# A two-layer backbone kernel on one core: work of the rounds moved from VectorE to GpSimd, convolution steps dealt out anew, two sets of weights placed elsewhere

## The chip, the core and the metric

The kernel runs on one core of one Trainium2 chip. Its five engines run side by side, each through its own list of instructions: TensorE (PE in the profile; its weight loads are PEld), VectorE (DVE), ScalarE (ACT), GpSimd (POOL) and SyncE (SP), which here issues nearly all DMA transfers. An instruction that needs another engine's result waits for a semaphore, and everything behind it on its engine waits with it.

The metric is the device time of one execution in microseconds. The kernel before takes 1331.81 us (median of three: 1330.71, 1331.81, 1332.05).

## The reference, cut to what matters

One sample: x is 1024 tokens by 1024 features, ctx 256 tokens by 1024. All inputs are 32-bit floats. Layer 0 works on x and on ctx, layer 1 on x alone.

```python
def even_mixer(h, h0, p):                        # layer 0
    z = h @ p["w_in"]                            # 1024 -> 5 x 1024
    va, vg, ga, xb, gb = jnp.split(z, 5, axis=-1)
    y_a = conformer_conv(va, vg, p) * silu(ga)
    y_b, hT = rglru_branch(xb, p, h0, True)
    y_b = y_b * silu(gb)
    return concatenate([y_a, y_b], -1) @ p["w_out"], hT

def conformer_conv(va, vg, p):
    u = va * sigmoid(vg)
    u = depthwise_conv(u, conv_w, conv_b)        # 31 taps along the tokens
    return silu(layernorm(u, ln_g, ln_b))        # over the features

def rglru_branch(xb, p, h0, with_outputs):
    u = depthwise_conv(xb, sconv_w, sconv_b)     # 4 taps
    # both directions: r, i = sigmoid(block-diagonal products of u)
    # a = exp(-8 r softplus(-lam)); b = sqrt(1 - a^2) * i * u
    # h[t] = a[t] h[t-1] + b[t]; y = forward h + backward h

# layer 0: x = x + gate * even_mixer(modulate(rmsnorm(x)), states of ctx)
# layer 1: a pooling mixer with gates; then a last rmsnorm
```

## The kernel before, in words

**Layout.** Features lie on the 128 partitions, tokens along the free axis, so 1024 features are eight tiles j = 0 to 7 of 128 x 1024. Halves of 512 tokens (h = 0, 1) are the unit of one PSUM bank. ctx adds 256 columns to the tiles of the recurrent branch, hence the shapes 128x1280.

**Products.** Each float32 factor is split into a high part (a cast on ACT; names with h, as `wh_vg`, `ybh`, `uh`) and a low part (value minus high part, a subtraction; names with l, as `wl_vg`, `ybl`, `ul`). A product is three matmul series, high by high, low by high and high by low. PE needs each low part one matmul after the high part, so a late low part stops it.

**What sets the order.** From the start of layer 0 to the end of its convolution branch every engine's order is written by hand: the helper `on` (L471 to L476) chains each instruction behind the one before it on its engine, and all of them carry the line L475 in the profile. Behind that (from L1147 on) a scheduler sets the order from its own estimate. The profile's lines tell the two apart.

**The rounds (L703 to L799).** Round j, for j = 0 to 7, takes 42.5 us. On PE: vg(j), va(j), the next tile's xb, the block-diagonal gate products `g`, all from the normalised input. On ACT the sigmoids, exponentials, square roots and the high parts of the weights. On GpSimd the low parts of the weights (`wl_vg`, `wl_va`, `wl_xb`, `wl_gw`) and the element products of the recurrence (`l<-l,uc`, `l<-l,l`). On DVE the four-tap convolution of xb (`uc<-xb,sm,uc`), u = va * sigmoid(vg), the scans of the tile before (`rec_scan`: an element-wise step and two scans for each direction, all `l<-l,l`), the sum of both directions (`rec_sum`, 128x1024), and the long convolution.

**The long convolution** of tile j (`conv(j)`) is a generator of some 50 steps, most of them one SCALAR_TENSOR_TENSOR over half the tokens ("a tap"). Its two accumulators `conv` lie in PSUM banks; the rows with `wsum` use sums of neighbouring tokens (`cL`, made by `spread_sum`, or in place for j of 5 and more). The eight tiles have 395 steps. They have no place of their own: `fill(n)` puts the next n steps at the point of the DVE order where it is called. When a tile is done, `ln_sums` adds it to `lnsum`, two 128x512 additions, for the mean of the layernorm. Before the change a full round calls for 30 steps, the gap behind the last round for 26, the gated tiles for 46, and what is then left runs in the stretch of the wob products.

**Last scans (L836 to L851).** Products gb1 to gb3 run on PE while the last tile is scanned; the low part of the weights gb4 is made on DVE between the two scans.

**Gated tiles (L982 to L1008).** For each tile n and half h: `yr` (the recurrence's output, from DRAM) times the silu of gb (`sb`) on DVE, the high part `ybh` on ACT, the low part `ybl` on GpSimd, then some taps on DVE. `gb_weights(j + 2)` puts a weight's load, cast and low part between tiles: gb5 to gb7, then the first two of w_out's lower half (`wob` 0 and 1).

**wob products (L1061 to L1091).** For m = 0 to 7, two halves each: 48 matmuls over the eight gated tiles. m = 0 takes tiles 0 to 6 of both halves first, then tile 7. Behind each half DVE has `fill(7)`. After m = 5 PE takes the layernorm's mean, a product of `lnsum` with ones (`mu`, `ln_mean`), for which all eight convolutions must be done; at m = 6 and 7 DVE centres the tiles, adds up squares, and PE makes `ms_ln`.

**ya and woa (L1147 on).** Scheduled: the gate products ga, the multiplication with u, four combinations of quarters (`ya_t1`, `ya_t2`, `ya_b11`, `ya_b21` and three more), and then w_out's upper half by a scheme of seven products of quarters in place of eight (`quad`, L937ff: in order b11, t1, t2, b21, t3, b22, t4, with psum names qa, qc, qb). Its weights are combined likewise in `wquad` (loads `wr_woa`, sums `ws_woa` and L912, L913, L919, splits `wq_woa`).

## Time and profile before

| | |
|---|---|
| median of three runs | 1331.81 us |
| the profiled execution's own time | 1331.6 us |
| its span (first to last instruction) | 1329.8 us |
| mean granted clock of TensorE | 0.986 |
| TensorE busy | 1282.6 us, 96% of the span, 5600 matmuls |
| VectorE busy | 1139.7 us, 86%, 1771 instructions |
| ScalarE busy | 631.0 us, 47% |
| GpSimd busy | 320.6 us, 24%, 172 instructions |

How to read it. A row of the timeline gives the start in us from the span's start, the duration, the engine, the line, the operation and its tiles (out<-in), the shape, "xN" where N like rows follow each other and are shown as one, and in brackets how long the engine had been idle before it and what ended that. Matmuls are pipelined: each is shown with 0.39 us, but at full clock they start 0.227 us apart, so it is the distance of the starts that counts on PE. The same goes for DVE and GpSimd, where a row's end overlaps the next row's start by about 0.08 us. In the table of windows each stretch of time has the busy time of PE, PEld, DVE, ACT and POOL with the number of instructions, the granted TensorE clock, the share of the DMA engines and GB/s.

### The profile page before, as it was taken

Reading aid. Unit: us, or ns where it says so; the run is one execution under the profiler, and the core shown is the slowest. Engines: PE = TensorE matmul, PEld = TensorE weight load, DVE = VectorE, ACT = ScalarE, POOL = GpSimd, SP = SyncE. Lnnn points to the kernel's source line nnn. Section 1 sums busy time; section 2 is a strip of 40 time slices with the busy share of each in tenths; the row PEclk is TensorE's granted clock in tenths of the full one; section 3 lists DMA queues with packets and bytes.
Section 4 is the critical chain, followed back from the end, with each engine's and each line's share of the span. In section 5 each row is a group of like instructions: output and inputs, shape, how many; then the busy total and the mean of one; then the engine's idle time right before and its main releaser. Section 6 shows DMA issues by size and latency. Waiting matters only on the chain. (4 is left out here: it accounts for less than half of the span.)

```text
span 1329.8 us, 15728 instructions
## 1 busy us (share of the span) xinstructions
PE 1282.6 (96%) x5600; PEld 1026.3 (77%) x5600; DVE 1139.7 (86%) x1771; ACT 631.0 (47%) x919; POOL 320.6 (24%) x172
## 2 busy tenths in 40 slices
...
GB/s 360 345 117 145 56 55 49 56 56 72 40 64 51 100 107 125 172 96 80 167 190 182 120 192 188 88 127 151 118 112 111 117 113 166 261 222 256 214 100 127
DMA packets 82867, 181.80 MB, mean 137 GB/s; under 512 B 7778, under 2 KB 27618, under 8 KB 82788
## 3 DMA queue, kind: packets, MB, share of 16 engines
...
HBM read 136.72 MB, written 44.04 MB: 136 GB/s over the span
## 5 line engine op out<-in xcount | busy, mean ns | idle before, releaser
L475 DVE SCALAR_TENSOR_TENSOR conv<-u,sm,conv 128x505 f32<-128x505 f32 (+6 forms) x224 | 153.1, 746 | 0.8
L1582 POOL TENSOR_TENSOR o<-x,rr 128x256 f32<-128x256 f32 (+1 forms) x9 | 8.0, 927 | 460.6 <-ACT rr L1570 460.6
L475 ACT ACTIVATE l<-g,sm 128x512 f32<-128x512 f32 (+1 forms) x96 | 58.7, 619 | 57.8 <-PE g L475 56.0
L281 PE MATMUL fold<-graw,wu 128*128 128x512 f32 x128 | 57.4, 609 | 1.6 <-DMA wu<-wu 1.6
L475 POOL TENSOR_TENSOR l<-l,l 128x1280 f32<-128x1280 f32 x16 | 47.1, 2961 | 26.1 <-DVE conv L475 21.1
L475 PE MATMUL wob<-ybl,wh_wob 128*128 128x512 f32 x128 | 50.6, 395 | 2.4 <-POOL ybl L475 2.4
L475 PE MATMUL wob<-ybh,wh_wob 128*128 128x512 f32 x128 | 51.6, 403 | 0.0
L281 PEld LDWEIGHTS fold<-graw,wu 128*128 128x128 f32 x128 | 24.8, 195 | 33.5 <-issue 29.6
L475 PE MATMUL wob<-ybh,wl_wob 128*128 128x512 f32 x128 | 50.4, 394 | 0.0
L475 PE MATMUL gb<-h0l,wh_gb 128*128 128x512 f32 x128 | 49.8, 389 | 0.0
L475 PE MATMUL gb<-h0h,wh_gb 128*128 128x512 f32 x128 | 49.8, 389 | 0.0
L475 PE MATMUL vg<-h0h,wh_vg 128*128 128x512 f32 x128 | 49.8, 389 | 0.0
L475 PE MATMUL vg<-h0h,wl_vg 128*128 128x512 f32 x128 | 49.8, 389 | 0.0
L475 PE MATMUL vg<-h0l,wh_vg 128*128 128x512 f32 x128 | 49.8, 389 | 0.0
L475 PE MATMUL va<-h0h,wh_va 128*128 128x512 f32 x128 | 49.8, 389 | 0.0
L475 PE MATMUL va<-h0l,wh_va 128*128 128x512 f32 x128 | 49.8, 389 | 0.0
L475 PE MATMUL va<-h0h,wl_va 128*128 128x512 f32 x128 | 49.8, 389 | 0.0
L475 PE MATMUL gb<-h0h,wl_gb 128*128 128x512 f32 x128 | 49.8, 389 | 0.0
L102 ACT CAST wq_g<-wr_g 128x512 fp32r<-128x512 f32 x48 | 28.2, 620 | 45.1 <-DVE wr_g L912 18.3
L475 DVE TENSOR_TENSOR_SCAN l<-l,l 128x256 f32<-128x256 f32 (+1 forms) x32 | 48.7, 1521 | 1.1
L102 ACT CAST wq_wo<-wr_wo 128x512 fp32r<-128x512 f32 x48 | 28.9, 620 | 40.5 <-DMA wr_wo<-wo 13.8
L475 DVE SCALAR_TENSOR_TENSOR conv<-cL,wsum,conv 128x506 f32<-128x506 f32 (+3 forms) x70 | 47.6, 746 | 0.2
...
## 6 DMA issues: line engine op xcount, KB each, us to landing
...
```

The lines of the kernel that those rows point to most:

```text
L102: return (nc.scalar.copy(hi, src), eng.tensor_tensor(out=lo, in0=src, in1=hi.bitcast(F32), op=sub))
L281: nc.tensor.matmul(ps, w[:, kc], gs[i], start=(i == 0), stop=(i == 3))
L475: last[eng] = f(*args, **kw)
L1582: nc.gpsimd.tensor_tensor(out=o[:, k - k0], in0=v, in1=rr, op=mult)
```

## The change

Five edits. **(1)** In the rounds three groups of SBUF-only work go from DVE to GpSimd: `ul`, the low part of the convolved tile, in all eight rounds; `rec_sum` in seven rounds (the last stays on DVE); and the `ln_sums` of tiles that end within the rounds, which are now called ahead of `rec_exp`. `at_rest` (the `cL` sums) is called before the scans and no longer calls `ln_sums`. **(2)** The calls of `fill` in a round go from 2, 2 and 4 to 3, 4 and 8 (5 in the last round); 10, 6 and 3 stay. **(3)** At the last scans `fill(24)` becomes `fill(15)`, and `ln_sums` follows `rec_sum`. **(4)** The low parts `ybl` go from GpSimd to DVE, with one tap between the cast's input and the subtraction; the taps behind each half go from 2, 2, 4, 4, 4, 4, 3, 0 to 1, 1, 2, 2, 2, 2, 1, 0, so that with the new tap the gated tiles have 38 instead of 46; and the weights wob 1 come behind tile 6 instead of ahead of it. **(5)** `wquad_begin` starts the weights of the first woa block ahead of the last ga product: both loads, the sums and two splits there, the other splits at the old place.

```diff
@@ -581,11 +581,14 @@
     ended, summed, spread_ = [0], [1], [0]
     NSPREAD = 5
 
-    def ln_sums():
+    def vadd(**kw):
+        return vec(nc.vector.tensor_tensor, **kw)
+
+    def ln_sums(by=vadd):
         for j in range(summed[0], ended[0]):
             for h in range(2):
                 first = us[0][:, HALF[h]] if j == 1 else lnacc[h][:, :H]
-                vec(nc.vector.tensor_tensor, out=lnacc[h][:, :H], in0=first, in1=us[j][:, HALF[h]], op=add)
+                by(out=lnacc[h][:, :H], in0=first, in1=us[j][:, HALF[h]], op=add)
         summed[0] = max(summed[0], ended[0])
 
     def edge_sum(j):
@@ -604,7 +607,6 @@
         return cL[:, HALF[j % 2]]
 
     def at_rest():
-        ln_sums()
         while spread_[0] < min(whole_[0], ended[0] + 2, NSPREAD):
             spread_sum()
 
@@ -679,9 +681,9 @@
             vec(nc.vector.tensor_tensor_scan, out=iu[:, lat], data0=at[:, lat], data1=iu[:, lat],
                 initial=first, op0=mult, op1=add)
 
-        def rec_sum(st):
+        def rec_sum(st, by):
             hs, hb = st[2][1], st[2][3]
-            vec(nc.vector.tensor_tensor, out=hs[:, C:], in0=hs[:, C:], in1=hb[:, C:], op=add)
+            by(out=hs[:, C:], in0=hs[:, C:], in1=hb[:, C:], op=add)
             nc.sync.dma_start(yb_raw[st[0]], hs[:, C:])
 
 
@@ -718,7 +720,7 @@
             all_of(mm3_fixed(vg[0], w, (hh, hl), HALF[0]))
             if state is not None:
                 rec_input(state, 1)
-            fill(2)
+            fill(3)
             first_tap(j, xb, uc[:, C:])
             other_taps(j, xb, uc[:, C:], 1)
             if state is not None:
@@ -730,8 +732,8 @@
             uh, ul = utile(f"uh{j}", F32R), utile(f"ul{j}", F32R)
             cast(uh, uc)
             act(sg[1], vg[1], AF.Sigmoid)
-            fill(2)
-            vec(nc.vector.tensor_tensor, out=ul, in0=uc, in1=uh.bitcast(F32), op=sub)
+            fill(4)
+            gp(out=ul, in0=uc, in1=uh.bitcast(F32), op=sub)
             name = "gb0" if final else f"xb{j + 1}"
             wnext = raw_split(raw_load(win[4 * KT] if final else win[3 * KT + j + 1], name), name)
             gwh, gwl = [tpool.tile([P, H], F32R, tag="t", name=f"w{n}_gw{j}") for n in "hl"]
@@ -748,6 +750,7 @@
                 vec(nc.vector.tensor_tensor, out=m0[:, 0, 2 * KT :], in0=m0[:, 0, 2 * KT :],
                     in1=col(O_MB + 2 * KT, KT), op=add)
             if state is not None:
+                ln_sums(gp)
                 rec_exp(state)
                 rec_root(state)
                 for d in range(2):
@@ -773,11 +776,11 @@
             fill(3)
             if not final:
                 other_taps(j + 1, xc, ucn[:, :C])
+            at_rest()
             if state is not None:
                 for d in range(2):
                     rec_scan(state, d)
-                rec_sum(state)
-            at_rest()
+                rec_sum(state, gp)
             xb = wide(name if final else f"xb{j + 1}")
             steps = (x for h in range(2) for x in mm3_fixed(xb[:, HALF[h]], wnext, (hh, hl), HALF[h]))
             if state is None:
@@ -795,7 +798,7 @@
                     w = raw_split(raw, name)
                     rec_input(now, 0)
             all_of(steps)
-            fill(19 if state is None else 4)
+            fill(19 if state is None else 5 if final else 8)
             state, uc = now, ucn
 
 
@@ -838,7 +841,7 @@
         gb_silu(0)
         gb_silu(1)
         gb_product(3, gws[3])
-        fill(24)
+        fill(15)
         rec_scan(state, 0)
         raw = raw_load(win[4 * KT + 4], "gb4")
         hi = wpool.tile([P, D], F32R, tag="wh", name="wh_gb4")
@@ -847,7 +850,8 @@
         vec(nc.vector.tensor_tensor, out=lo, in0=raw, in1=hi.bitcast(F32), op=sub)
         gws[4] = hi, lo
         rec_scan(state, 1)
-        rec_sum(state)
+        rec_sum(state, vadd)
+        ln_sums()
         at_rest()
 
     cpool.release()
@@ -889,6 +893,34 @@
     loaded = [None]
 
 
+
+    def wquad_begin(src, name, ring):
+        raw = []
+        for i in range(2):
+            r = wpool.tile([P, D], F32, tag="wr", name=f"wr_{name}_{i}")
+            loaded[0] = nc.sync.dma_start(r, src[i])
+            raw.append(r)
+        a11, a12 = [raw[0][:, h] for h in HALF]
+        a21, a22 = [raw[1][:, h] for h in HALF]
+
+        def op(v, i):
+            t = ring(f"wq_{name}_{i}")
+            split(v, t[:, HALF[0]], t[:, HALF[1]], nc.vector)
+            return t
+
+        s3 = ttile(f"ws_{name}")
+        nc.vector.tensor_tensor(out=s3, in0=a11, in1=a21, op=sub)
+        nc.vector.tensor_tensor(out=a21, in0=a21, in1=a22, op=add)
+        p1, p5 = op(a11, 1), op(a21, 5)
+        nc.vector.tensor_tensor(out=a11, in0=a21, in1=a11, op=sub)
+
+        def rest():
+            p6, p2, p7 = op(a11, 6), op(a12, 2), op(s3, 7)
+            nc.vector.tensor_tensor(out=a12, in0=a12, in1=a11, op=sub)
+            p3 = op(a12, 3)
+            return p1, p2, p3, op(a22, 4), p5, p6, p7
+
+        return rest
 
     def wquad(src, name, ring, late=False):
         raw = []
@@ -986,25 +1018,28 @@
             nc.sync.dma_start(y, yb_raw[n][:, HALF[h]])
             vec(nc.vector.tensor_tensor, out=y, in0=y, in1=sbs[n][h], op=mult)
             cast(th[:, HALF[h]], y)
-            gp(out=tl[:, HALF[h]], in0=y, in1=th[:, HALF[h]].bitcast(F32), op=sub)
+            fill(1)
+            vec(nc.vector.tensor_tensor, out=tl[:, HALF[h]], in0=y, in1=th[:, HALF[h]].bitcast(F32), op=sub)
             fill(between)
         bh.append(th)
         bl.append(tl)
 
     gb_product(4, gws[4])
-    gated(0, 2)
+    gated(0, 1)
     gb_silu(2)
     gb_weights(5)
     gb_product(5, gws[5])
-    gated(1, 2)
+    gated(1, 1)
     for j in range(3, KT + 1):
         if j < KT:
             gb_silu(j)
-        if 3 < j < KT:
+        if 3 < j < KT - 1:
             gb_weights(j + 2)
         if 3 < j < KT - 2:
             gb_product(j + 2, gws[j + 2])
-        gated(j - 1, (0, 0, 4, 4, 4, 4, 3, 0)[j - 1])
+        gated(j - 1, (0, 0, 2, 2, 2, 2, 1, 0)[j - 1])
+        if j == KT - 1:
+            gb_weights(j + 2)
         ln_sums()
 
 
@@ -1140,6 +1175,14 @@
 
     mods = mod_halves()
 
+    ring_n = 0
+
+    def ring_w(name):
+        nonlocal ring_n
+        tag = ("wh", "wl", "d", "d")[ring_n % 4]
+        ring_n += 1
+        return dtile(name, F32R) if tag == "d" else wpool.tile([P, D], F32R, tag=tag, name=name)
+
     ya = {}
     for name in BOPS[:4]:
         operand(ya, name, d2tile, "ya")
@@ -1147,6 +1190,8 @@
     for i in range(KH):
         for j in (i, KH + i) if i else ():
             w = wload(win[2 * KT + j], f"ga{j}", nc.gpsimd)
+            if j == KT - 1:
+                w0 = wquad_begin([wout[q, 0] for q in range(2)], "woa0", ring_w)
             for h in range(2):
                 ps = psum(f"ga{j}_{h}")
                 mm3(ps, w, (hh, hl), HALF[h])
@@ -1169,18 +1214,10 @@
         for _ in range((6, 6, 4, 0)[i]):
             next(mods)
 
...
-    w0 = wo_weights(0)
+    w0 = w0()
     for name in BOPS[4:]:
         operand(ya, name, dtile, "ya")
         for i in range(KH):
```

Three places where instructions move. First, GpSimd in round 4, from `wl_va` to the next tile's `wl_vg`; `l<-l,l` with 128x1280 are the recurrence's products, and numbers behind names are the program's own. Before:

```order
L475 TENSOR_TENSOR wl_va_2109<-wr_va_2106,wh_va_2108 128x1024
L475 TENSOR_TENSOR wl_xb_2149<-wr_xb_2146,wh_xb_2148 128x1024
L475 TENSOR_TENSOR wl_gw_2153<-wr_gw_2154,wh_gw_2152 128x512
L475 TENSOR_TENSOR l_658<-l_658,l_653 128x1280
L475 TENSOR_TENSOR l_657<-l_657,l_654 128x1280
L475 TENSOR_TENSOR wl_vg_2369<-wr_vg_2235,wh_vg_2368 128x1024
```

With the change:

```order
L475 TENSOR_TENSOR wl_va_2133<-wr_va_2130,wh_va_2132 128x1024
L475 TENSOR_TENSOR ul_2164<-uc_1949,uh_2163 128x1280
L475 TENSOR_TENSOR wl_xb_2175<-wr_xb_2172,wh_xb_2174 128x1024
L475 TENSOR_TENSOR wl_gw_2179<-wr_gw_2180,wh_gw_2178 128x512
L475 TENSOR_TENSOR l_658<-l_658,l_653 128x1280
L475 TENSOR_TENSOR l_657<-l_657,l_654 128x1280
L475 TENSOR_TENSOR l_658<-l_658,l_657 128x1024
L475 TENSOR_TENSOR wl_vg_2398<-wr_vg_2262,wh_vg_2397 128x1024
```

`ul` now stands ahead of `wl_xb`, and the 128x1024 sum of both directions between the recurrence's products and `wl_vg`.

Second, the last gated tiles: GpSimd before, from tile 5's second low part to tile 7's (`wl_wob` are the low parts of the weights wob 0 and wob 1):

```order
L475 TENSOR_TENSOR ybl_3937<-yr_1_3948,ybh_3936 128x512
L475 TENSOR_TENSOR wl_wob_3968<-wr_wob_3965,wh_wob_3967 128x1024
L475 TENSOR_TENSOR ybl_3972<-yr_0_3973,ybh_3971 128x512
L475 TENSOR_TENSOR ybl_3972<-yr_1_3981,ybh_3971 128x512
L475 TENSOR_TENSOR ybl_3990<-yr_0_3991,ybh_3989 128x512
L475 TENSOR_TENSOR ybl_3990<-yr_1_3996,ybh_3989 128x512
```

DVE with the change, tile 6 (`yr_0_3998`) and the first half of tile 7:

```order
L475 TENSOR_TENSOR yr_0_3998<-yr_0_3998,sb_0_3962 128x512
L475 SCALAR_TENSOR_TENSOR conv_0_3694<-u_2870,wsum 128x512
L475 TENSOR_TENSOR ybl_3997<-yr_0_3998,ybh_3996 128x512
L475 SCALAR_TENSOR_TENSOR u_2870<-u_2870,sm,conv_1_3695 128x512
L475 TENSOR_TENSOR yr_1_4005<-yr_1_4005,sb_1_3963 128x512
L475 SCALAR_TENSOR_TENSOR conv_1_3695<-u_2870,wsum,conv_1_3695 128x511
L475 COPY conv_1_3695<-edges 128x1
L475 TENSOR_TENSOR ybl_3997<-yr_1_4005,ybh_3996 128x512
L475 SCALAR_TENSOR_TENSOR conv_0_3694<-u_2870,wsum,conv_0_3694 128x505
L475 TENSOR_TENSOR yr_0_4021<-yr_0_4021,sb_0_3992 128x512
L475 SCALAR_TENSOR_TENSOR conv_1_3695<-u_2870,wsum,conv_1_3695 128x506
L475 TENSOR_TENSOR ybl_4020<-yr_0_4021,ybh_4019 128x512
```

The low parts of tile 6 stood on GpSimd behind those of wob 1; they now stand on DVE, one tap behind the product that they come from.

Third, DVE ahead of the first woa block, from the sum behind t1 on. `u*ga` is L1155 before and L1200 now, the sums of the weights L911 to L919 before and L912 to L919 now. Before:

```order
L103 TENSOR_TENSOR ya_t1l_4873<-u_1831,ya_t1h_4871 128x512
L1155 TENSOR_TENSOR u_3158<-u_3158,ga_0_5351 128x512
L103 TENSOR_TENSOR ya_b21l_4881<-u_3158,ya_b21h_4879 128x512
L1155 TENSOR_TENSOR u_3158<-u_3158,ga_1_5378 128x512
L1162 TENSOR_TENSOR u_1831<-u_3158,u_1831 128x512
L1163 TENSOR_TENSOR yat_3_5409<-u_3158,u_1831 128x512
L911 TENSOR_TENSOR ws_woa_5425<-wr_woa_0_5418,wr_woa_1_5420 128x512
L1164 TENSOR_TENSOR u_3158<-u_3158,yat_3_5409 128x512
L912 TENSOR_TENSOR wr_woa_1_5420<-wr_woa_1_5420 128x512
L103 TENSOR_TENSOR ya_t2l_4877<-yat_3_5409,ya_t2h_4875 128x512
L103 TENSOR_TENSOR wq_woa_7_5438<-ws_woa_5425,wq_woa_7_5438 128x512
L913 TENSOR_TENSOR wr_woa_0_5418<-wr_woa_1_5420,wr_woa_0_5418 128x512
```

With the change:

```order
L103 TENSOR_TENSOR wq_woa_5_5361<-wr_woa_1_5353,wq_woa_5_5361 128x512
L1200 TENSOR_TENSOR u_3210<-u_3210,ga_0_5365 128x512
L103 TENSOR_TENSOR ya_t1l_4873<-u_1853,ya_t1h_4871 128x512
L103 TENSOR_TENSOR wq_woa_6_5432<-wr_woa_0_5351,wq_woa_6_5432 128x512
L103 TENSOR_TENSOR wq_woa_2_5435<-wr_woa_0_5351,wq_woa_2_5435 128x512
L103 TENSOR_TENSOR wq_woa_4_5445<-wr_woa_1_5353,wq_woa_4_5445 128x512
L103 TENSOR_TENSOR ya_t3l_5450<-u_847,ya_t3h_5448 128x512
L103 TENSOR_TENSOR ya_t3l_5450<-u_1172,ya_t3h_5448 128x512
L919 TENSOR_TENSOR wr_woa_0_5351<-wr_woa_0_5351 128x512
L103 TENSOR_TENSOR ya_b21l_4881<-u_3210,ya_b21h_4879 128x512
```

The two sums that open the weights (`ws_woa`, L913) and the third (L915) stand ahead of the first of these rows now, wq_woa_5 ahead of the last tile's products, and the weights 6, 2 and 4 with two low parts of t3 ahead of `ya_b21l`; the products that end in `ya_t2l` come later. On PE the first block's steps of b11 and t1 keep their places; then came two steps of t2, two of b21 and ten of t2, and now come nine of t2, twelve of b21, two of the next block's b11, one of t2 and twelve of b22.

6 lines of the change are left out of this document (removed).

## The prediction

> **What bounds the kernel now.** PE is busy 96% of the span, so I read the table of PE's waits first, then the windows, which tell in which stages PE works without a gap, then the timelines around the longest waits.
>
> ```profile
> PE mu L475 <- DVE lnsum L475: 10.1, 1, 10.1
> ...
> PE qc_woa L931 <- ACT wq_woa L102: 2.5, 1, 2.5
> PE wob L475 <- POOL ybl L475: 2.4, 1, 2.4
> ```
>
> ```profile
> core 0: us, PE busy (x) PEld busy (x) DVE busy (x) ACT busy (x) POOL busy (x), PEclk, DMA share, GB/s
> ...
> 245.00:290.00 45.00, 45.00 (x223) 38.20 (x223) 41.81 (x57) 26.46 (x30) 22.68 (x10) 1.00 0.15 53
> ...
> 706.00:760.00 54.00, 51.00 (x212) 41.15 (x211) 44.04 (x71) 25.70 (x47) 0.00 (x0) 0.94 0.52 176
> ```
>
> Each of the three waits occurs once and lies where the change works. In the window of a round PE has no gap at all: nothing is to be won there, only lost. DVE is idle for 45.00 - 41.81 = 3.2 us of it, GpSimd for 22.3 us. So the rounds can carry more of DVE's work, if it stays inside those idle times.
>
> What each wait costs is read from the starts of matmuls, since the clock falls behind a stop. First wait, the gated tiles' low part:
>
> ```profile
> 513.73 0.39 PE L475 MATMUL wob<-ybh,wh_wob 128*128 128x512 f32 x1
> 516.49 0.50 PE L475 MATMUL wob<-ybl,wh_wob 128*128 128x512 f32 x1 [2.37 <-POOL ybl L475]
> ...
> 517.77 0.63 PE L475 MATMUL wob<-ybh,wh_wob 128*128 128x512 f32 x1
> ...
> 521.16 0.40 PE L475 MATMUL wob<-ybh,wl_wob 128*128 128x512 f32 x1
> ```
>
> There are 14 steps from 513.73 to 521.16, 7.43 us. At 0.227 us a step (further down, 609.08 to 609.31) they take 3.18. Loss: **4.25 us**, of which 2.5 is the stop and the rest the slow steps from 517.77 to 521.16, eight of them in 3.39 us.
>
> Second wait, the mean of the layernorm:
>
> ```profile
> 578.99 0.39 PE L475 MATMUL wob<-ybh,wl_wob 128*128 128x512 f32 x1
> 589.51 3.60 PE L475 MATMUL mu<-lnsum,ones 128*128 128x512 f32 x4 [10.14 <-DVE lnsum L475]
> ...
> 593.19 0.39 PE L475 MATMUL wob<-ybl,wh_wob 128*128 128x512 f32 x1
> ...
> 609.08 0.39 PE L475 MATMUL wob<-ybh,wl_wob 128*128 128x512 f32 x1
> 609.31 1.02 PE L475 MATMUL ms_ln<-lnsum,ones 128*128 128x512 f32 x2
> ...
> 610.39 0.39 PE L475 MATMUL wob<-ybl,wh_wob 128*128 128x512 f32 x1
> ```
>
> From 578.99 to 593.19 are 14.20 us. Undisturbed, four products with ones cost what the two `ms_ln` show, twice: 610.39 - 609.31 less one step is 0.85, so 1.70, and two steps make 2.15. Loss: **12.05 us**. DVE has no idle time before it:
>
> ```profile
> 578.38 8.59 DVE L475 SCALAR_TENSOR_TENSOR conv<-u,wsum,conv 128x505 f32<-128x505 f32 x13
> ...
> 588.77 1.29 DVE L475 TENSOR_TENSOR lnsum<-lnsum,u 128x512 f32<-128x512 f32 x2
> ```
>
> The taps come too late by amount, not by order: 8.59 / 13 = 0.66 us each.
>
> Third wait, the first woa weights:
>
> ```profile
> 704.40 0.69 DVE L1155 TENSOR_TENSOR u<-u,ga 128x512 f32<-128x512 f32 x1 [1.79 <-ACT ga L1153]
> ...
> 705.74 0.69 DVE L1163 TENSOR_TENSOR yat<-u,u 128x512 f32<-128x512 f32 x1
> ...
> 707.54 0.68 DVE L912 TENSOR_TENSOR wr_woa<-wr_woa 128x512 f32<-128x512 f32 x1
> ```
>
> ```profile
> 706.08 0.39 PE L934 MATMUL qa_woa<-ya_b11h,wq_woa 128*128 128x512 f32 x1
> 708.93 0.79 PE L931 MATMUL qc_woa<-ya_t1h,wq_woa 128*128 128x512 f32 x1 [2.46 <-ACT wq_woa L102]
> ...
> 715.55 0.47 PE L933 MATMUL qb_woa<-ya_t2l,wq_woa 128*128 128x512 f32 x1
> ```
>
> 14 steps in 9.47 us instead of 3.18: loss **6.3 us**. The sum that the weights wait for (L912) stands on DVE behind the last tile's products, which wait for ACT's silu. All three together: 22.6 us, and that is the most the change can win.
>
> **The change part by part.** *Rounds.* The rows of round 4, first GpSimd, then DVE, then PE:
>
> ```profile
> 264.09 2.41 POOL L475 TENSOR_TENSOR wl_vg<-wr_vg,wh_vg 128x1024 fp32r<-128x1024 f32 x1 [14.37 <-DVE conv L475]
> ...
> 272.29 2.41 POOL L475 TENSOR_TENSOR wl_va<-wr_va,wh_va 128x1024 fp32r<-128x1024 f32 x1
> 279.14 2.41 POOL L475 TENSOR_TENSOR wl_xb<-wr_xb,wh_xb 128x1024 fp32r<-128x1024 f32 x1 [4.43 <-ACT wh_xb L475]
> ...
> 286.32 5.88 POOL L475 TENSOR_TENSOR l<-l,l 128x1280 f32<-128x1280 f32 x2 [3.52 <-DVE conv L475]
> ```
>
> ```profile
> 260.03 1.23 DVE L475 TENSOR_TENSOR l<-l,l 128x1024 f32<-128x1024 f32 x1
> 261.17 1.29 DVE L475 TENSOR_TENSOR lnsum<-u,u 128x512 f32<-128x512 f32 x2
> ...
> 274.75 1.49 DVE L475 TENSOR_TENSOR ul<-uc,uh 128x1280 fp32r<-128x1280 f32 x1
> ```
>
> ```profile
> 266.90 0.39 PE L475 MATMUL vg<-h0h,wl_vg 128*128 128x512 f32 x1
> ```
>
> On DVE go, start to start, 1.40 for `ul` (1.49 less the overlap of 0.09), 1.14 for the sum of directions, and 1.2 for `lnsum` in a little over half of the rounds, 0.7 on average: 3.2 us. Seven taps more cost 7 x 0.66 = 4.6. Net +1.4 us a round, against 3.2 us idle: it fits, with 1.8 to spare.
>
> On GpSimd come 2.94 for `ul` (half of 5.88, the same shape), 2.4 for the 128x1024 sum (as `wl_vg`), and at times 2 x 1.29 (`ybl`, 128x512, below, is two in 2.97 or less). `ul` fits between the end of `wl_va` (274.70) and 279.14, where GpSimd idles 4.43; the `lnsum` pair fits into the 3.52 ahead of 286.32. The sum of directions begins when DVE's scans end, 260.03, and would end at 262.4, ahead of `wl_vg`'s start at 264.09: 1.7 us of slack. Behind it is the narrowest place of the change: `wl_vg` ends at 266.50 and PE wants it at 266.90. Lateness of the scans beyond about 2.1 us reaches PE. DVE carries four taps more at a round's end (2.6 us) and three in its first part, less `ul`; its small waits in a round take up most, and I expect scans 0 to 2 us late. Cost taken: **+0.3 us**; bounds 0, and seven stops like the first wait, 7 x 4.25 = 29.8.
>
> Taps: +46 in the rounds (22 stays 22, six of 30 become 37, 30 becomes 34), -9 at the last scans, -8 at the gated tiles: 29 fewer are left for the wob products, 19.1 us of DVE.
>
> *Last scans.*
>
> ```profile
> 455.27 1.05 ACT L475 CAST wh_gb<-wr_gb 128x1024 fp32r<-128x1024 f32 x1 [6.45 <-issue]
> ```
>
> ```profile
> 456.35 1.23 DVE L475 TENSOR_TENSOR wl_gb<-wr_gb,wh_gb 128x1024 fp32r<-128x1024 f32 x1 [0.42 <-ACT wh_gb L475]
> ```
>
> DVE waits here for ACT's cast, and that waited for a buffer which PE's gb products hold. With nine taps fewer the first scan is done sooner and DVE only waits longer. Value 0, PE has no gap here; the 6 us are idle time bought.
>
> *Gated tiles.*
>
> ```profile
> 511.52 3.23 POOL L475 TENSOR_TENSOR wl_wob<-wr_wob,wh_wob 128x1024 fp32r<-128x1024 f32 x1 [1.40 <-ACT wh_wob L475]
> 514.71 2.97 POOL L475 TENSOR_TENSOR ybl<-yr,ybh 128x512 fp32r<-128x512 f32 x2
> ```
>
> Tile 6's low parts stood 3.23 us behind the weights of wob 1. On DVE they follow the cast by one tap (0.66), and the cast no longer follows that of wob 1. I put tile 6 at about 512 where PE wants it at 513.95, tile 7's halves at 517 and 519 against 519.2 and 520.1. DVE gets 16 subtractions at 0.6 (9.6 us) and loses 8 taps (5.3). The wait that can take the old one's place is tile 7's: `wl_wob` may run beside it and hold it up, as it did here:
>
> ```profile
> 494.63 2.39 POOL L475 TENSOR_TENSOR wl_gb<-wr_gb,wh_gb 128x1024 fp32r<-128x1024 f32 x1 [0.62 <-ACT wh_gb L475]
> ```
>
> ```profile
> 485.47 0.74 DVE L475 SCALAR_TENSOR_TENSOR conv<-u,sm,conv 128x505 f32<-128x505 f32 x1
> ...
> 494.83 2.74 DVE L475 TENSOR_TENSOR yr<-yr,sb 128x512 f32<-128x512 f32 x1
> ```
>
> The product `yr<-yr,sb`, both inputs in SBUF, took 2.74 instead of 0.69 and ended after GpSimd's row; a tap with its accumulator in PSUM is not held up. Gain: **-3.7** of 4.25; bounds 0 and 4.25.
>
> The Trainium skill, "SBUF — State Buffer", section "Who interferes with whom", says that a VectorE instruction with two SBUF inputs and a GpSimd instruction that reads SBUF exclude each other for their whole length, and one with a single SBUF input does not. The rows at 494.83 and 485.47 agree. The rule speaks against edit 1: were each added GpSimd row to block DVE for its length, a round would lose DVE 5.3 us more and 3.2 us of idle time would not hold that. Most of DVE's time there is taps, which the rule lets pass.
>
> *wob.* DVE's end at 590 comes 19.1 us earlier, to 571. The 4.3 us that the subtractions cost net come on top only as far as they don't fall into DVE's waits for the loads of `yr`, 7.2 us in all: 571 to 575.
>
> ```profile
> DVE yr L475 <- DMA yr<-yb_raw: 7.2, 5, 3.1
> ```
>
> PE, freed of the first wait, wants `mu` at 579.2 - 3.7 = 575.5. Gain: **-12.0**; bounds -12.05 and, were the taps shifted by only half, about -6.
>
> *woa.* The sums now stand ahead of the last tile's products, in idle time like the 1.79 at 704.40. In their place t2's last part gets later: between the rows of `ya_t1l` and `ya_t2l` DVE has 25 rows instead of 8, 13 of the 17 ahead of `yat`, the product that t2 is cast from. 13 x 0.6 less the 1.79 idle puts `yat` at 705.74 + 6.0 = 711.7, and its cast behind others on ACT at 713 or so. PE's order asks for it later too: from 703.59 (706.08 less eleven steps) come 24 steps of b11 and t1, nine of t2, twelve of b21, two of the next block's b11, 47 x 0.227 = 10.7 us, so at 714.3; for the low part twelve steps of b22 later. The margin is under 2 us, and the next block's first weight must have come by DMA by 713.8. Gain: **-5.0**, the stop mostly gone and a small one kept; bounds 0 (the wait moves on whole) and -6.3.
>
> Sum: 1331.6 + 0.3 - 3.7 - 12.0 - 5.0 = 1311.2; the median lies 0.2 above the profiled execution: **1311**. Of itself the likeliest case reaches from 1308 to 1315.
>
> The Trainium skill, "TensorE: Matmul & The Clock Gate", Part 1, "What's actually happening", has the clock halved after an idle window of about 3.4 us. Here a stop of 2.37 us was enough (0.43 a step from 517.77). By the rule the first wait would be worth 2.5 and not 4.25, and the sum 1313; the row decides.
>
> **The rivals.** *A, only the mean's wait goes (1319).* Tile 7's low parts meet `wl_wob`, and in the woa block the last t2 or the next weights are late. For it: 494.83, and a full DVE at both. Against it: both needs come later than the old ones. 1331.8 - 12.0 - 1 = 1319.
>
> *B, the woa wait moves on (1315).* The first block's weights are early, but the 17 rows pushed ahead of `ya_t2l`, or the next block's load, stop PE once, for 2 us with slow steps behind it: 1311 + 4. For it: a margin under 2 us, and DVE busy 44.04 of 54 us in that window. Against it: the order on PE that puts 23 other steps ahead of the last t2.
>
> *C, GpSimd stops PE in the rounds (about 1341).* Place: the sum of directions ahead of `wl_vg`, in seven rounds. Price: a stop of 2.4 us costs 4.25, seven of them 29.8: 1311 + 30. It decides from scans ending 4.5 us later than at 260.03, and the case is slower than before from 20.6 / 7 = 2.9 us a round. For it: the margin of 0.4 at 266.90. Against it: DVE's 1.8 us to spare.
>
> *D, the taps do not come off (1323).* The added taps and subtractions run into waits, and DVE reaches the mean's end as late as before; only the other two waits go: 1331.8 - 8.7. Against it: 3.2 us idle a round.
>
> **How the numbers follow.** Forecast 0.62, A 0.13, B 0.12, C 0.06, D 0.04, and 0.03 for nothing won. The range takes in A and B and the forecast's own low end, which cannot pass 1331.8 - 22.6 = 1309 by much: 1307 to 1320. About 0.2% (2.7 us) can be told from no change. Faster 0.91, same 0.03, slower 0.06.
>
> **What would show it.** Right: PE's waits no longer list `mu` or `ybl`; DVE's last convolution row ends before 575; windows of the rounds keep PE full; the qc rows follow the qa rows at 0.227. The rounds are wrong if PE waits for `wl_vg` from GpSimd; the gated step if PE waits for `ybl` from DVE at tile 7; the woa step if a wait for `ya_t2l` or `wq_woa` stands within 10 us behind. A time above 1320 would mean a wait that I have not placed.

## The result, and the profile after

| | before | after |
|---|---|---|
| median | 1331.8 us | 1317.21 us |
| lowest to highest | 1330.71 to 1332.05 | 1315.32 to 1318.11 |
| profiled execution, its span | 1331.6, 1329.8 | 1316.52, 1314.7 |
| granted TensorE clock | 0.986 | 0.994 |

The ratio is 0.989, 95% interval 0.9873 to 0.9907: 14.6 us won, where 20.8 had been forecast. The time lies in the stated range and outside what the likeliest case allowed by itself.

Where the 15.1 us of the two spans came from is read from PE. Its order is the same in both up to the woa blocks, so a matmul has the same place in both traces, and the difference of its starts, taken at the stage's two ends, is what a stage won or lost:

| stage on PE | forecast | measured |
|---|---|---|
| start to the second round's first vg | 0 | +1.08 |
| from there to the last round's first vg | +0.3 | +0.29 |
| last round, gb products, to the first wob matmul | 0 | +0.69 |
| first wob product (48 matmuls) | -3.7 | -0.91 |
| wob 1 to 5 | 0 | +0.03 |
| the mean | -12.0 | -12.03 |
| to the first woa matmul | 0 | +0.01 |
| the woa blocks | -5.0 | -5.04 |
| everything behind | 0 | +0.79 |
| sum | -20.4 | -15.08 |

The woa blocks are followed to the first `fold` matmul, with which the next product begins. Three terms came out to a tenth of a microsecond. One, the gated tiles, did not. The table of PE's waits of the changed kernel shows which wait stands there now, and that of DVE's waits shows who waits for the mean:

```profile
PE wob L475 <- ACT ybh L475: 1.6, 2, 1.0
...
PE wob L475 <- DVE ybl L475: 0.4, 2, 0.2
```

```profile
DVE u L475 <- PE mu L475: 8.9, 1, 8.9
```

**The mean.** DVE had its last sum done at 570.17 + 2.40 = 572.6, PE came at 580.40 without a gap behind its last wob matmul. Now DVE waits for PE, 8.9 us:

```profile
580.17 0.39 PE L475 MATMUL wob<-ybh,wl_wob 128*128 128x512 f32 x1
580.40 1.88 PE L475 MATMUL mu<-lnsum,ones 128*128 128x512 f32 x4
```

```profile
570.17 2.40 DVE L475 TENSOR_TENSOR lnsum<-lnsum,u 128x512 f32<-128x512 f32 x2
581.45 2.48 DVE L475 TENSOR_TENSOR u<-u,mu 128x512 f32<-128x512 f32 x4 [8.89 <-PE mu L475]
```

**The first woa block.** The t1 product follows the b11 product at a step's distance, and what is left is one short stop at t2, for a copy on ACT:

```profile
695.25 0.39 PE L966 MATMUL qa_woa<-ya_b11h,wq_woa 128*128 128x512 f32 x1
695.48 0.39 PE L963 MATMUL qc_woa<-ya_t1h,wq_woa 128*128 128x512 f32 x1
...
698.78 0.50 PE L963 MATMUL qb_woa<-ya_t2h,wq_woa 128*128 128x512 f32 x1 [0.42 <-ACT qb_woa L979]
```

**The gated tiles.** PE, then DVE, then GpSimd around tile 7, which is the last in the first wob product:

```profile
516.16 0.50 PE L475 MATMUL wob<-ybl,wh_wob 128*128 128x512 f32 x1
...
522.70 0.50 PE L475 MATMUL wob<-ybh,wh_wob 128*128 128x512 f32 x1 [1.04 <-ACT ybh L475]
523.43 0.50 PE L475 MATMUL wob<-ybl,wh_wob 128*128 128x512 f32 x1 [0.22 <-DVE ybl L475]
...
524.68 0.50 PE L475 MATMUL wob<-ybh,wh_wob 128*128 128x512 f32 x1 [0.52 <-ACT ybh L475]
525.41 0.50 PE L475 MATMUL wob<-ybl,wh_wob 128*128 128x512 f32 x1 [0.23 <-DVE ybl L475]
```

```profile
515.41 0.69 DVE L475 TENSOR_TENSOR ybl<-yr,ybh 128x512 fp32r<-128x512 f32 x1
...
519.39 2.61 DVE L475 TENSOR_TENSOR yr<-yr,sb 128x512 f32<-128x512 f32 x1
...
522.68 0.69 DVE L475 TENSOR_TENSOR ybl<-yr,ybh 128x512 fp32r<-128x512 f32 x1
523.29 0.69 DVE L475 TENSOR_TENSOR yr<-yr,sb 128x512 f32<-128x512 f32 x1
```

```profile
519.05 2.40 POOL L475 TENSOR_TENSOR wl_wob<-wr_wob,wh_wob 128x1024 fp32r<-128x1024 f32 x1 [10.69 <-ACT wh_wob L475]
```

Tile 6's low part (DVE 515.41, PE 516.16) no longer stops PE for more than a fraction of a microsecond. But GpSimd began the low part of the weights wob 1 at 519.05, 0.34 us ahead of tile 7's first product, which then took 2.61 us instead of 0.68. PE stopped four times, 2.0 us in sum, and behind each pair of stops the next matmul also starts later than a step (0.34 us instead of 0.227).

**The rounds.** The narrow place is where it was said to be. Round 1 to 2, GpSimd and PE:

```profile
178.30 2.41 POOL L475 TENSOR_TENSOR l<-l,l 128x1024 f32<-128x1024 f32 x1 [12.46 <-DVE l L475]
180.66 2.40 POOL L475 TENSOR_TENSOR wl_vg<-wr_vg,wh_vg 128x1024 fp32r<-128x1024 f32 x1
```

```profile
182.79 0.39 PE L475 MATMUL vg<-h0l,wh_vg 128*128 128x512 f32 x1
183.12 0.50 PE L475 MATMUL vg<-h0h,wl_vg 128*128 128x512 f32 x1
...
435.55 0.50 PE L475 MATMUL gb<-h0h,wl_gb 128*128 128x512 f32 x1
```

`wl_vg` ended at 183.06, and PE took it at 183.12, a tenth after its turn (0.227 behind 182.79). The same thing at the last round's end cost 0.4 at 435.55. The other 0.3 of the gap was lost at 490.27, where PE waited for the low part of a gb weight among the gated tiles; only the kernels with edit 4 lose anything there (e2 below does, e1 and e4 do not).

### The profile page after: what moved, and what is told of

Same layout as the page of the kernel before. It is cut to its first block, busy times and chain, and to the rows that moved or that the text cites. A ratio compares the mean times of both kernels' runs of the same rounds, so it can differ in the third digit from the quotient of the medians.

```text
span 1314.7 us, 15715 instructions
## 1 busy us (share of the span) xinstructions
PE 1279.6 (97%) x5600; PEld 1022.7 (78%) x5600; DVE 1137.1 (86%) x1764; ACT 632.3 (48%) x919; POOL 351.8 (27%) x179
## 4 chain that ended last, share of the span: by engine, by line
PE 59%; DVE 15%; DMA 9%; ACT 4%; issue 4%; POOL 2%; SPq 0%; POOLq 0%; DVEq 0%; ACTq 0%
PE vg L475 7%; PE wob L475 6%; PE xb L475 6%; PE va L475 6%; PE g L475 4%; PE ga L475 2%; PE ga L134 2%; PE ga L133 2%; PE ga L135 2%; DMA yr_t<-y_t 2%; PE xbc L475 2%; DVE ws L1340 1%; DMA x_part<-xp 1%; DMA wr_g<-wg 1%; DVE conv L475 1%
## 5 line engine op out<-in xcount | busy, mean ns | idle before, releaser
L475 POOL TENSOR_TENSOR l<-l,l 128x1280 f32<-128x1280 f32 (+1 forms) x23 | 64.0, 2796 | 92.0 <-DVE l L475 65.6
L103 POOL TENSOR_TENSOR wl_wu<-wr_wu,wh_wu 128x1024 fp32r<-128x1024 f32 x8 | 19.5, 2433 | 106.7 <-ACT wh_wu L102 105.9
```

What stands on the lines that cost most here:

```text
L103: eng.tensor_tensor(out=lo, in0=src, in1=hi.bitcast(F32), op=sub))
L475: last[eng] = f(*args, **kw)
```

## The experiments

Twelve runs were made, in four groups; the kernels of a group ran on one chip, beside the kernel before. Executions of one kernel spread by several us there (the kernel before: 1325.47 to 1335.09 on the first of these chips), so terms of one or two us are read from the stages on PE, and the medians decide only large ones. All stages are differences to the first profile of before, in us; "rounds" is second to last round, "gap" runs to the first wob matmul, "wob 0" is the first wob product. The stage from there to the mean is left out: it is within 0.1 of zero, except for +0.97 in e4, +1.06 in e5, +0.61 in e11 and +1.11 in e10.

| kernel | ratio to before, 95% interval | rounds | gap | wob 0 | mean | woa | behind |
|---|---|---|---|---|---|---|---|
| changed kernel | 0.9890 (0.9873 to 0.9907) | +0.29 | +0.69 | -0.91 | -12.03 | -5.04 | +0.79 |
| e5, changed again | 0.9872 (0.9848 to 0.9895) | +0.37 | +0.93 | -0.30 | -12.02 | -5.44 | -3.39 |
| e1, edits 1 to 3 | 0.9944 (0.9921 to 0.9967) | +0.32 | +0.41 | -1.16 | -12.02 | -0.11 | -0.25 |
| e2, edit 4 | 1.0062 (1.0037 to 1.0086) | 0.00 | +0.23 | -2.20 | +9.42 | -0.01 | -2.63 |
| e3, edit 5 | 0.9962 (0.9946 to 0.9978) | 0.00 | 0.00 | -0.11 | +0.32 | -5.09 | -4.93 |
| e4, all but edit 4 | 0.9887 (0.9863 to 0.9911) | +0.32 | +0.40 | +0.72 | -12.03 | -4.86 | +0.96 |
| e6, wob 1's low part on DVE | 0.9877 (0.9858 to 0.9896) | +0.37 | +0.76 | -2.03 | -12.03 | -5.53 | +0.16 |
| e11, tile 7 freed, old buffers | 0.9876 (0.9850 to 0.9901) | +0.37 | +0.63 | -1.37 | -12.02 | -5.45 | -1.81 |
| e7, tile 7 freed | 0.9839 (0.9822 to 0.9857) | +0.34 | +0.69 | -4.05 | -12.02 | -5.21 | -1.91 |
| e12, the same again | 0.9848 (0.9821 to 0.9875) | +0.36 | +0.60 | -3.97 | -12.02 | -4.89 | -0.99 |
| e8, and the sum behind wl_vg | 0.9858 (0.9840 to 0.9875) | +0.07 | +4.39 | -4.05 | -12.02 | -4.66 | -1.37 |
| e9, all but edit 1 | 1.0245 (1.0206 to 1.0284) | +35.56 | +15.07 | -0.92 | -12.03 | -4.66 | -3.05 |
| e10, all but edit 3 | 0.9888 (0.9854 to 0.9921) | +0.31 | +0.98 | -0.80 | -12.02 | -4.87 | +3.32 |

The last column, behind the woa blocks, goes from -4.93 to +3.32, and two profiles of the changed kernel alone differ in it by 4.18. No edit touches the code there, though the scheduler places some of its instructions differently. "Rounds" and "mean" repeat to 0.1. "Gap" and "wob 0", hand-written too, do not: between the two rows of the changed kernel they differ by 0.24 and 0.61. The gap is +0.4 with edits 1 to 3 and without edit 4 (e1, e4), +0.23 with edit 4 alone, and +0.6 to +1.0 with all of them (e8 and e9 apart).

### e1, edits 1 to 3 alone

```diff
-            vec(nc.vector.tensor_tensor, out=ul, in0=uc, in1=uh.bitcast(F32), op=sub)
+            gp(out=ul, in0=uc, in1=uh.bitcast(F32), op=sub)
...
-                rec_sum(state)
+                rec_sum(state, gp)
...
-            fill(19 if state is None else 4)
+            fill(19 if state is None else 5 if final else 8)
...
-        fill(24)
+        fill(15)
```

> The kernel before with edits 1, 2 and 3 alone (rounds and last scans); gated tiles and woa weights as before. Theory (the three waits are separate terms, and 29 fewer taps are left in the wob stretch in any case): the mean's wait goes whole, -12.05, the two late low parts in the rounds that the changed kernel shows (at 182 and 434 us) cost +0.9, the stop at ybl (4.25) and that at the woa weights (6.3) stay: 1320.7, between 1319.5 and 1322. Rival (the mean needs the gated edit too, because DVE only comes early if the gated tiles carry 38 taps and not 46): PE still waits for mu, 3 us or more, and the time is 1324 or above.

Median 1323.04 against 1330.26 of before. No wait for mu: the mean's term is -12.02 without edit 4, so the rival falls. The median lies 1.0 above the range that was expected; the profiled execution (1320.01) lies in it. The stop at the woa weights stayed (2.5 in PE's table), as expected, and the stage is -0.11. It is taken here to the same place in PE's order as in the other rows, since the scheduler put the first `fold` matmul twelve steps earlier in this kernel.

### e2, edit 4 alone

```diff
-            gp(out=tl[:, HALF[h]], in0=y, in1=th[:, HALF[h]].bitcast(F32), op=sub)
+            fill(1)
+            vec(nc.vector.tensor_tensor, out=tl[:, HALF[h]], in0=y, ...)
...
-        gated(j - 1, (0, 0, 4, 4, 4, 4, 3, 0)[j - 1])
+        gated(j - 1, (0, 0, 2, 2, 2, 2, 1, 0)[j - 1])
...
```

> The kernel before with edit 4 alone (low parts of the gated tiles on DVE, 38 taps there instead of 46, weights wob 1 behind tile 6). Theory (what edit 4 saves on PE at 516 us is 0.7, and DVE gets 16 subtractions of 0.6, 9.6 us, while the taps it drops there come back later): DVE reaches the mean later by 9.6 us less what falls into its 7.2 us of waits for the loads of yr, so the mean's wait grows by 2.4 to 9.6 and the kernel is slower than before, 1334 to 1341. Rival (the stop of 4.25 us at ybl is a term of its own that edit 4 takes away): 1328 to 1331.

Median 1339.38: slower than before, by 9.1 (the profiled one by 5.4, its part behind the woa blocks being 2.63 faster). PE's wait for the mean, before 10.1:

```profile
PE mu L475 <- DVE lnsum L475: 19.6, 1, 19.6
```

It grew by 9.5. Part of this is PE, which came 1.4 us earlier; the rest, 8.1, is DVE, most of the 9.6 of its 16 subtractions, so little fell into the waits for `yr`. Edit 4 is not a term of its own: without the taps moved elsewhere it wins 2.20 in the first wob product and costs more at the mean, most of what it puts on DVE.

### e3, edit 5 alone

```diff
+            if j == KT - 1:
+                w0 = wquad_begin([wout[q, 0] for q in range(2)], "woa0", ring_w)
...
-    w0 = wo_weights(0)
+    w0 = w0()
```

> The kernel before with edit 5 alone (first woa weights begun ahead of the last ga product). Theory: the stop at 708.93 goes and nothing takes its place, 5.0 to 6.3 us: 1325.5 to 1327, with no wait of PE for wq_woa over 0.5 us. Rival (the early loads only found their place because the mean's wait was gone, or the wait moves to the last t2 or the next weights): gain under 2.5 us, 1329.5 or above, and a wait for ya_t2l or wq_woa of 1 us or more within 10 us behind.

Median 1325.51, 4.75 below before; stage -5.09; PE's table has no wait for `wq_woa` or `ya_t2l`. The rival falls: the edit stands alone, and the mean's wait (10.1 here) has nothing to do with it.

### e4, the changed kernel without edit 4

> The changed kernel with edit 4 undone (low parts on GpSimd, 46 taps at the gated tiles, wob 1 ahead of tile 6), all else as changed. Theory (edit 4 only put a new wait at tile 7 in place of the one at tile 6, and the mean has slack: DVE waited 8.9 us for mu there): 0.7 slower than the changed kernel, 1317.9, within 1 us of it. Rival (edit 4 is worth its 4.25 us, and the missing gain went elsewhere): 1321 to 1322.

(The diff is that of e2, reversed.) Median 1315.88, ratio 0.9887 against 0.9890 of the changed kernel: undoing the edit costs nothing that can be measured. In the stage "wob 0" it is +0.72 against -0.91 and -0.30, while e1, with the same gated tiles, has -1.16. From the first wob matmul to the mean it is +1.69 here (0.97 of it behind the first product), -1.12 in e1, and -0.88 and +0.76 in the two profiles of the changed kernel. So edit 4 as it stands wins nothing that stands out of this spread, where 3.7 had been forecast. The loss that it was to take away varies too: in e1, with the old gated tiles, the stop at `ybl` is 1.5 us and no slow step follows, while before it was 2.37 with eight slow steps behind it.

### e5 and e6, what holds tile 7

e5 is the changed kernel again.

> The changed kernel once more, as the control for the three that follow on the same chip. Expected stage by stage on PE against the profile of before: rounds and gap +1.0 to +1.5, first half of the first wob product -0.5 to -1.5, mean -12.0, woa -5.0; whatever differs by more than 1 us ahead of the rounds or behind the woa blocks is spread of the chip, since the change has nothing there.

Median 1314.32; rounds and gap +1.30, as expected; "wob 0" -0.30, outside what was expected by 0.2, with tile 7's product again at 2.61 beside GpSimd's weights. The same four stops as in the first profile (2.0 and 2.1 us in sum) cost 1.06 more behind that product. The granted clock was 0.53 from 525 to 528 this time, and 1.00 there in the first profile:

```profile
524.65 0.80 PE L475 MATMUL wob<-ybl,wh_wob 128*128 128x512 f32 x1 [0.23 <-DVE ybl L475]
525.25 0.63 PE L475 MATMUL wob<-ybh,wl_wob 128*128 128x512 f32 x1
...
527.38 0.60 PE L475 MATMUL wob<-ybl,wh_wob 128*128 128x512 f32 x1
```

Five steps from 525.25 to 527.38 took 2.13 us; at 0.227 they take 1.13.

e6 makes the low part of wob 1 on DVE:

```diff
-        if j == KT - 1:
-            gb_weights(j + 2)
+        if j == KT - 1:              # load and cast as before; the subtraction:
+            late.append(lambda: vec(nc.vector.tensor_tensor, out=lo, in0=raw, in1=hi.bitcast(F32), op=sub))
...
+            if h and late:
+                late.pop()()
+            else:
+                fill(1)
```

> The changed kernel with the low part of the weights wob 1 made on DVE, between tile 7's second product and its low part in place of a tap, so that GpSimd has nothing to do beside tile 7. Theory (tile 7's first product yr took 2.61 instead of 0.69 because GpSimd's wl_wob ran beside it, and that made PE stop for ybh and ybl of the first half): yr takes 0.7, the stop of 1.04 for the first half is gone, the second half's stays, about 0.5 to 1, since its load is issued when tile 6's buffer comes free near 518.8 and lands 2.7 later; the first wob product ends 1 to 2 us earlier against the rounds than in the control. Rival (tile 7 is late because DVE has too much to do there): yr takes 0.7, but PE's stops stay 1.5 us or more in sum.

```profile
517.90 0.69 DVE L475 TENSOR_TENSOR yr<-yr,sb 128x512 f32<-128x512 f32 x1
...
520.32 0.69 DVE L475 TENSOR_TENSOR yr<-yr,sb 128x512 f32<-128x512 f32 x1 [0.35 <-DMA yr<-yb_raw]
```

```profile
521.72 0.50 PE L475 MATMUL wob<-ybh,wh_wob 128*128 128x512 f32 x1 [0.83 <-ACT ybh L475]
522.80 0.50 PE L475 MATMUL wob<-ybl,wh_wob 128*128 128x512 f32 x1 [0.58 <-DVE ybl L475]
```

With GpSimd idle the product took 0.69, and the first half's stops are gone; the second half's stayed, behind a product that waited for its load. Stage -2.03, 1.1 to 1.7 better than the two of the changed kernel: the theory holds, with half of the loss left over. The stops left (0.83 and 0.58, 1.41 in sum) lie just under the 1.5 at which the rival would have held. The median (1316.97) doesn't show so little.

### e7, e11 and e12, the other half

The tiles `yr` lie in a ring of two buffers, used in turn: a load can only be issued when the work on the half two places earlier is done. e7 also takes the second half of tile 7's `yr` from another ring of tiles, so that its load doesn't wait for a buffer of tile 6, and puts both products first:

```diff
...
+        for h in range(2):
+            y = vtile(f"yr{n}_{h}") if h == 0 else ttile(f"yr{n}_{h}")
+            nc.sync.dma_start(y, yb_raw[n][:, HALF[h]])
+            vec(..., out=y, in0=y, in1=sbs[n][h], op=mult)
+            cast(th[:, HALF[h]], y)
...
+        cast(hi, raw)                # weights wob 1
+        for h in range(2):
+            vec(..., out=tl[:, HALF[h]], in0=ys[h], in1=th[:, HALF[h]].bitcast(F32), op=sub)
+        vec(..., out=lo, in0=raw, in1=hi.bitcast(F32), op=sub)
...
```

> As before this, and tile 7's second half of yr in another ring of tiles, so that its load doesn't wait for tile 6's buffer; both products of tile 7 first, then both low parts, then the weights' low part, with no taps between, and one tap fewer behind tile 6. Theory (GpSimd's lock and the buffer of yr are the two things that hold tile 7): no stop of PE over 0.3 us in the first wob product apart from tile 6's, which is below 0.5: 2.5 to 3.5 us better than the control from the first wob matmul to the 49th. Rival (a later wait takes over: the weights wob 1 or 2 come late): a stop for wl_wob or wh_wob of over 1 us at m = 1 or 2, and under 1.5 us better.

```profile
517.59 1.29 DVE L475 TENSOR_TENSOR yr<-yr,sb 128x512 f32<-128x512 f32 x2 [0.89 <-DMA yr<-yb_raw]
```

PE has no stop left in the stage: -4.05, of the 4.25 lost in the kernel before, and nothing came late behind it. That is 3.1 to 3.75 better than the two profiles of the changed kernel, where 2.5 to 3.5 had been expected. Median 1310.45 beside 1314.32 for the changed kernel on the same chip.

e11 takes e7's order, but the old ring (`vtile` for both halves).

> The kernel with tile 7 freed, but tile 7's second half of yr back in the ring of two buffers, so that its load waits for tile 6's second low part again. This separates the order (both products first, no taps between) from the buffer. Theory (order and lock made the gain, and without the taps the buffer comes free early enough): load issued near 516.7, landing near 519.6, so one stop of PE for the second half of at most 0.5 us; first wob product within 1 us of the kernel with tile 7 freed (-4.05 against before in that stage, so -3.0 to -4.0). Rival (the buffer is what holds the second half, as the stops of 0.83 and 0.58 for it showed where only GpSimd's lock was gone): -2.0 to -2.7.

```profile
523.09 0.69 DVE L475 TENSOR_TENSOR yr<-yr,sb 128x512 f32<-128x512 f32 x1 [3.44 <-DMA yr<-yb_raw]
```

```profile
524.44 0.50 PE L475 MATMUL wob<-ybl,wh_wob 128*128 128x512 f32 x1 [2.25 <-DVE ybl L475]
```

Here I was wrong and the rival's mechanism right, with a loss larger than its range (-2.0 to -2.7): the stage is -1.37. The load of the second half was issued at 518.37, when tile 6's second low part was done and its buffer free, and landed at 523.00. These 4.6 us are longer than the 2.8 of the same load in e7; why is open. Two things held tile 7, GpSimd's row and the ring of two buffers. Taking away GpSimd's row, alone (e6) or with the new order (e11), brings less than half; no run takes away the ring alone.

> The kernel with tile 7 freed once more, timed for a narrower interval. Theory (3 to 4 us better than the changed kernel, all of it in the first wob product): 1310 to 1313, ratio to before 0.983 to 0.986, and again no stop of PE there. Rival (the better median of the first time was spread of the chip in the parts behind, which no edit touches): ratio 0.987 or above.

e12 repeats e7: stage -3.97, no stop, median 1310.73, ratio 0.9848 (0.9821 to 0.9875). This is the version that beats both kernels: both medians are below the lowest run of the changed kernel on any chip (1312.70), though the intervals of the ratios overlap.

### e8, the sum of directions behind wl_vg

```diff
                     w = raw_split(raw, name)
+                    if state is not None:
+                        rec_sum(state, gp)
                     rec_input(now, 0)
...
-                rec_sum(state, gp)
```

> As before this, and in the rounds the sum of both directions (rec_sum) behind wl_vg on GpSimd instead of ahead of it. Theory (PE lost 0.2 to 0.4 in some rounds and 0.7 in the gap since wl_vg and wl_gb stood behind that sum): rounds and gap at most +0.3 against before, so 3.5 to 4.5 better than the control in all. Rival (the sum, 2.4 later, holds up its store and the tiles that the next round reuses, so ACT's halving and the products behind it come later): PE stops for g or wl_va in the rounds, +1 or more.

In the rounds the theory's 0.3 came (+0.07 instead of +0.34). The rival's loss came too, though not in the rounds, where it had put it, but in the gap: +4.39 instead of +0.69.

```profile
PE gb L475 <- POOL wl_gb L475: 3.4, 2, 2.0
```

```profile
434.20 2.85 POOL L475 TENSOR_TENSOR l<-l,l 128x1024 f32<-128x1024 f32 x1
```

```profile
437.08 1.37 ACT L475 ACTIVATE l<-l,chalf 128x1280 f32<-128x1280 f32 x1 [3.35 <-POOL l L475]
439.76 1.37 ACT L475 ACTIVATE l<-l,chalf 128x1280 f32<-128x1280 f32 x1 [1.31 <-DMA yb_raw<-l]
```

The sum began at 434.20, ACT's halving behind it waited 3.35 us for it and 1.31 for its store, and the gb weights on GpSimd came late. The sum's place in the changed kernel, ahead of `wl_vg`, is the better of the two.

### e9, the taps without the moves

```diff
-            gp(out=ul, in0=uc, in1=uh.bitcast(F32), op=sub)
+            vec(nc.vector.tensor_tensor, out=ul, in0=uc, in1=uh.bitcast(F32), op=sub)
...
-                ln_sums(gp)
...
-                rec_sum(state, gp)
+                rec_sum(state, vadd)
+            ln_sums()
```

> The changed kernel with edit 1 undone: ul, rec_sum and ln_sums of the rounds on DVE again, the added taps of edit 2 and edits 3 to 5 kept. Theory (DVE has 3.2 us idle in a round, the seven taps take 4.6, so without the moves it falls behind by 1.4 a round): PE stops in the rounds, for g, ul or the like, +5 to +15 us between the first vg and the first wob, and the time is 1319 to 1329; the mean's wait stays away or small. Rival (PSUM tiles between the engines take up DVE's lateness, and the taps could have been added without moving anything): rounds at most +2, time as the changed kernel's.

Median 1362.51, +35.56 in the rounds and +15.07 in the gap: the direction of the theory, several times its size. Up to the fifth round PE lost 1.3 us; from there it lost 11 to 12 a round. DVE and GpSimd around 270, and the window behind (busy time of PE, PEld, DVE, ACT and POOL, then the granted clock):

```profile
267.35 3.22 DVE L475 TENSOR_TENSOR l<-l,l 128x1024 f32<-128x1024 f32 x1
270.49 6.82 DVE L475 TENSOR_TENSOR lnsum<-u,u 128x512 f32<-128x512 f32 x2
...
293.62 3.36 DVE L475 TENSOR_TENSOR ul<-uc,uh 128x1280 fp32r<-128x1280 f32 x1
```

```profile
269.44 7.32 POOL L475 TENSOR_TENSOR l<-l,uc 128x1280 f32<-128x1280 f32 x2
```

```profile
290.00:335.00 45.00, 37.50 (x163) 30.75 (x162) 44.62 (x49) 26.13 (x30) 23.65 (x8) 0.89 0.14 47
```

The sums that take 1.23 and 1.29 undisturbed (before: 260.03 and 261.17) took 3.22 and 6.82, `ul` 3.36 instead of 1.49. Once DVE is late, its rows with two SBUF inputs run beside GpSimd's `l<-l,uc` and weights instead of in the gap between them, and wait while GpSimd works: 1.99 + 5.53 + 1.87 = 9.4 us of one round's 11.6. What a microsecond of lateness costs is not constant here: it moves the next rows into a collision. The Trainium skill, "SBUF — State Buffer", section "Who interferes with whom", gives exactly this exclusion; the rows agree, and they show the size that it can reach.

### e10, 24 taps kept at the last scans

```diff
-        fill(15)
+        fill(24)
```

> The changed kernel with edit 3 undone: 24 taps at the last scans instead of 15. Theory (DVE's first scan there waits for GpSimd's products in any case, 4.21 instead of 1.49 us at 448.00 and the two scans 5.16 instead of 3.08, so nine taps, 5.9 us, fall into time that it loses anyway): the low part of gb4 on DVE starts within 1 us of the changed kernel's 458.1, PE reaches the first wob matmul within 0.5 us of it, and the time is the same. Rival (the nine taps push the gated tiles back by their 5.9 us): first wob matmul or tile 6 and 7 later by 2 us or more.

The changed kernel, GpSimd and then DVE:

```profile
444.97 5.88 POOL L475 TENSOR_TENSOR l<-l,l 128x1280 f32<-128x1280 f32 x2 [0.79 <-ACT l L475]
```

```profile
448.00 4.21 DVE L475 SCALAR_TENSOR_TENSOR l<-l,l 128x1280 f32<-128x1280 f32 x1
452.24 5.16 DVE L475 TENSOR_TENSOR_SCAN l<-l,l 128x256 f32<-128x256 f32 x2
458.13 1.23 DVE L475 TENSOR_TENSOR wl_gb<-wr_gb,wh_gb 128x1024 fp32r<-128x1024 f32 x1 [0.74 <-ACT wh_gb L475]
```

DVE in e10:

```profile
452.20 1.49 DVE L475 SCALAR_TENSOR_TENSOR l<-l,l 128x1280 f32<-128x1280 f32 x1
453.72 3.08 DVE L475 TENSOR_TENSOR_SCAN l<-l,l 128x256 f32<-128x256 f32 x2
456.72 1.20 DVE L475 TENSOR_TENSOR wl_gb<-wr_gb,wh_gb 128x1024 fp32r<-128x1024 f32 x1
```

Started later, the scan step and the scans took their plain 1.49 and 3.08. The low part of gb4 began 1.4 us earlier than in the changed kernel, outside the 1 us that was expected; but in this profile PE and ACT's cast came 1.4 to 1.7 earlier too, so against them it hardly moved. PE lost 0.98 in the gap against 0.69 and 0.93, and the time is the same (1315.08). Edit 3 is worth nothing that can be measured; the six us of taps fit into time that DVE otherwise lost, most of it beside GpSimd's rows.

## Why the prediction was right, and where not

**Right, by its own steps.** The mean: DVE's end was put at 571 to 575 and came at 572.6; the term was -12.0 and measured -12.03, and e1 shows it alone. The woa weights: -5.0, measured -5.04, and -5.09 alone in e3; the margin of under 2 us at the last t2 held, with 0.4 left (the cast on ACT ended at 703.70, PE took it at 704.12). The rounds: +0.3, measured +0.29, at the place named (`wl_vg` behind the sum, in one round 0.24). That the last two agree to a few hundredths is luck: both sizes were chosen between bounds and not worked out, and the woa stage goes from -4.66 to -5.53 in the kernels with edit 5. Last scans: value 0, shown by e10, though not for the reason given. DVE's wait for ACT's cast only grew from 0.42 to 0.74; what took up the time were the scan step and the scans, slow beside GpSimd's rows.

**The term that was mis-sized: the gated tiles, -3.7, measured -0.91 and -0.30.** The step that failed is "tile 7's halves at 517 and 519". They came at 523.4 and 525.3, and tile 6, put at 512, at 516.1. PE's first wob matmul was itself 2.06 later than before, so its needs for tile 7 moved as much, to 521.3 and 522.2; the rest is lateness of DVE. Tile 7's collision with `wl_wob` cost 1.93; the text named it as the wait that can take the old one's place, and then charged 0.55 for everything that might be left. The sign that it gave for a wrong gated step came: PE waits for `ybl` from DVE at tile 7. Two earlier low parts, now on DVE, had each lost 1.43 to GpSimd's weights in the same way:

```profile
498.78 2.12 DVE L475 TENSOR_TENSOR ybl<-yr,ybh 128x512 fp32r<-128x512 f32 x1
...
506.79 2.12 DVE L475 TENSOR_TENSOR ybl<-yr,ybh 128x512 fp32r<-128x512 f32 x1
```

Two rows would have been needed: when the weights of wob 1 are cast, now behind tile 6, and when tile 7's product runs. Both follow tile 6's last cast, so they fall close together. And the prediction did not look at the ring of two buffers for `yr` at all. The sign was a row in the profile of before, where tile 7's product waits 2.64 us for its load (e11 shows what it can cost):

```profile
519.90 0.69 DVE L475 TENSOR_TENSOR yr<-yr,sb 128x512 f32<-128x512 f32 x1 [2.64 <-DMA yr<-yb_raw]
```

**Rival A** came half true: its mechanism at tile 7, as it was written, but not its second half, since the woa wait did not move on. With A's first half alone the sum is 1331.8 - 12.0 - 5.0 - 0.9 + 0.3 = 1314.2; the rest to 1317.2 is +0.69 in the gap, and spread (+1.08 ahead of the second round and +0.79 behind the woa blocks, where the second profile of the same kernel has -0.15 and -3.39, and the median over the profiled execution). The gap had been put at 0. Some 0.4 of it is a low part of weights behind the sum of directions, at the last round, of the kind that was priced in the rounds; e1 and e4 have it too. The rest comes with edit 4 (490.27).

**Rival B and D** fall by e3 and e1. **Rival C** did not happen, and its price is not tested, since no run makes the scans late with the sum on GpSimd. e9 shows only that a DVE which falls behind costs over 11 us a round, not 4.25; its waits lie elsewhere in the main (from 290 to 430 us PE waits 8.1 us for `g` and 10.2 for the xb weights, 2.1 for `wl_vg`). The forecast that DVE's net +1.4 us a round fits into 3.2 us of idle time was right (DVE is busy 42.77 of 45 us in the window from 245 now, 0.96 more than before).

**The two rules that were weighed.** The row beat the rule for the clock in the kernel before: a stop of 2.37 brought steps of 0.43, with a granted clock of 0.50 from 518 to 521. The experiments add that no one length decides. A stop of 2.25 us in e11 brought no slow step (granted clock 1.00), and the changed kernel's four stops of at most 1.04 brought some in e5 and none in the first profile; what decides stays open. The other would have put 5.3 us more on DVE in a round, each added GpSimd row holding it up for its length. DVE is 0.96 us busier and still has 2.2 us idle in the window, so these rows did not.
